# A softmax ranked behind the values of an older block, and two product steps moved ahead of two transposes

## The chip, the cores and the metric

The kernel runs on one core of a Trainium2 chip. Its time is the time of one execution on the device in microseconds (us); several runs are made and their median is compared. One further execution is recorded by the hardware profiler, and the rows below come from that one.

## The reference

The program is a transformer trunk of two layers on 1024 tokens of width 1024, in float32. Layer 0 is gated retention. Layer 1, which the change touches, is gated differential attention with 8 heads: each head has two queries and two keys per token (64 numbers each) and one value (128 numbers). Cut to that layer:

```python
h  = rmsnorm(x, pre_norm[1])
kv = rmsnorm(x, kv_norm) @ w_kv           # two keys and one value per head
k, v = rope(kv[..., :1024]), kv[..., 1024:]
q, gate = rope((h @ w_in_b)[..., :1024]), (h @ w_in_b)[..., 1024:]
# per head, per block of 128 queries; keys of later 64-token chunks are masked
p = softmax(where(mask, q_t @ k_t.T / 8, -big))        # t = 0, 1
o = (p[0] - lam * p[1]) @ v
o = rmsnorm(o, sub_norm) * (1 - lambda_init)
x = x + rmsnorm((o * silu(gate)) @ w_out_b, post_norm[1])
```

## The kernel before

Every product of an activation with a weight is made as three matmuls on operands that are split into a high and a low part (`split` makes them: ScalarE writes the high part, L87 or L90, VectorE subtracts, L88 or L91; `mm3` issues the three matmuls, L100). Layer 1 begins about two thirds into the run.

Its main loop goes over 64 units, heads outside (8), blocks of 128 tokens inside (8). A unit projects q, k and v of its block: eight slabs of three matmuls with 384 columns (`gemm_piece`, L100, the tile `pq` in the "g" banks of PSUM). Then `rotate_b` applies the rotary tables: two products on VectorE (L566, L567), their sum on GpSimd (L568), and ScalarE copies v (L569). The unit also carries, in between its slabs, work of earlier blocks:

- behind slab 1, piece 0 of the attention, `scores` of the block two units back: matmuls with 64 rows for both score sets (L591) into the two buffers of PSUM tag "s2". A block b has (b + 1) x 128 keys, so block 5 has 768, block 6 has 896 and block 7 has 1024. In the same function stands the softmax: for each of the two score sets a memset of the masked corner (L597), the maximum on VectorE (L598) and the exponential on ScalarE (L599, with its sum); then reciprocal, factor and the combination of both sets (L601, L602, L604).
- behind slab 3, piece 1, `values` of the block scored two units earlier: matmuls of the turned weights with v (L627) into a buffer of tag "s", which ScalarE copies out with a scale (L630) and squares (L631); L105 on VectorE and L106 on GpSimd make the inverse root, L633 applies it, L634 stores the result.
- behind slab 4, `transpose_b`: two transposes of the q and k of the unit before (L577) into tag "s", which are split into `qk` (L87, L88); the next unit's scores read them.
- behind slabs 5 and 7, pieces 2 and 3, `turn` of the block scored one unit earlier: transposes of its weights (L616) into tag "s", copied by ScalarE (L617).

Tag "s" has two buffers, so the four pieces that use it pass them on to each other; tag "s2" has two, which the two score sets of one block fill.

`ahead` asks for weight slabs of the next head, at slab 0 of the units of blocks 1 to 4, and at slabs 0 to 3 of the unit of block 7; each is a load, two splits on ScalarE (L90) and two on VectorE (L91), into 12 buffers that the current head's slabs leave one by one. In the last head `load_wob` loads the output weights instead, whose splits are 1024 wide.

What sets the order on the engines: the library's planner goes through the instructions before the run and puts each on its engine's queue when it reckons it ready; among those that are ready together the one that the code asks for first goes first. On the chip the queues then run in that order. Buffers are handed on when their last reader has finished.

After the loop comes the output product: `outs` yields after each of its steps, a step being three matmuls of 512 columns; 16 steps make 128 rows of the output, eight steps for each bank of tag "g". Some steps are taken before the last `transpose_b`, then three after each remaining piece of the attention, and the rest at the end:

```python
    og_ = outs()
    for _ in range(4):
        next(og_)
    transpose_b(*prev)
    for step in att:
        for p in step:
            p()
            for _ in range(3):
                next(og_, None)
```

Of the kernel before, what the change touches and what calls it, by code (L numbers as in the profile page):

```python
# [35 lines left out]
def yoco_kernel(ctx: ExitStack, tc: tile.TileContext, a: dict):  # L36
# [16 lines left out]
    def sbuf(tag, shape, dt, nm):  # L53
        return sb.tile(shape, dt, name=f"{nm}_{next(uid)}", tag=tag, bufs=BUFS[tag])
# [13 lines left out]
    def kt(shape, nm, dt=F32):  # L68
        return sbuf("k", shape, dt, nm)

    def sm(n):
        return sbuf("m", [P, n], F32, "m")
# [3 lines left out]
    def ps(tag, n=512):  # L76
        return psum.tile([P, n], F32, name=f"p{tag}_{next(uid)}", tag=tag, bufs=PB[tag])
# [25 lines left out]
    def rsqrt(out, in_, mul, add, n=1):  # L103
        t = sm(n)
        nc.vector.tensor_scalar(out=t, in0=in_, scalar1=mul, scalar2=add, op0=ALU.mult, op1=ALU.add)  # L105
        nc.gpsimd.tensor_tensor(out=out, in0=t, in1=mhalf[:, 0:n], op=ALU.pow)  # L106
# [295 lines left out]
    for i in range(H * NC):  # L402
# [3 lines left out]
        u = {"h": h, "c": c, "wg": wg, "pp": ps("s2", 1024)}  # L406
# [174 lines left out]
    def scores(u):  # L581
        h, b, nk = u["h"], u["b"], u["nk"]
        q, qs = groups[h, b // 4][0][:, 0], slice(b % 4 * P, b % 4 * P + P)
        sc = [ps("s2", 1024) for t in range(2)]
        for c0 in range(0, nk, 512):
            n = min(512, nk - c0)
            k = groups[h, c0 // 512][0][:, 1]
            for i, (ql, kl) in enumerate(((0, 0), (0, 1), (1, 0))):
                for t in range(2):
                    rows = slice(t * 64, t * 64 + 64)  # L590
                    nc.tensor.matmul(  # L591
                        sc[t][:, c0 : c0 + n], q[rows, ql, qs], k[rows, kl, 0:n], start=(i == 0), stop=(i == 2)
                    )
        nm, s_ = sm(2), sm(2)
        pr = [kt([P, D], f"pr{t}") for t in range(2)]
        for t in range(2):
            nc.vector.memset(sc[t][0:64, nk - 64 : nk], NEG)  # L597
            nc.vector.tensor_reduce(out=nm[:, t : t + 1], in_=sc[t][:, :nk], axis=AX.X, op=ALU.max, negate=True)  # L598
            nc.scalar.activation(pr[t][:, :nk], sc[t][:, :nk], AF.Exp, bias=nm[:, t : t + 1], accum_out=s_[:, t : t + 1])  # L599
        rc, cf = sm(2), sm(1)  # L600
        nc.vector.reciprocal(rc, s_)  # L601
        nc.vector.tensor_scalar(out=cf, in0=s_[:, 0:1], scalar1=rc[:, 1:2], scalar2=nlam, op0=ALU.mult, op1=ALU.mult)  # L602
        w = pr[0][:, :nk]
        nc.vector.scalar_tensor_tensor(out=w, in0=pr[1][:, :nk], scalar=cf, in1=w, op0=ALU.mult, op1=ALU.add)  # L604
        u.update(w=w, rc=rc)

    def turn(u, i):
        w = u["w"]
        if i == 0:
            u["wT"] = kt([P, D], "wT")  # L610
        k0, k1 = i * 512, min(u["nk"], i * 512 + 512)
        if k0 >= k1:
            return
        pt = ps("s")
        for k in range(k0, k1, P):
            nc.tensor.transpose(pt[:, k - k0 : k - k0 + P], w[:, k : k + P], ident)  # L616
        nc.scalar.activation(u["wT"][:, k0:k1], pt[:, : k1 - k0], AF.Copy)  # L617
# [3 lines left out]
    def values(u):  # L621
        h, b, wT, rc = u["h"], u["b"], u["wT"], u["rc"]
        valued.add((h, b))
        po = ps("s", P)
        for kb in range(b + 1):
            v = groups[h, kb // 4][1]
            nc.tensor.matmul(po, wT[:, kb * P : (kb + 1) * P], v[:, kb % 4], start=(kb == 0), stop=(kb == b))  # L627
        o = sbuf("u", [P, 2, P], F32, "o")
        sq, r = sm(1), sm(1)
        nc.scalar.activation(o[:, 0], po, AF.Copy, scale=rc[:, 0:1])  # L630
        nc.scalar.activation(o[:, 1], o[:, 0], AF.Square, accum_out=sq)  # L631
        rsqrt(r, sq, 1.0 / P, EPS)
        nc.gpsimd.tensor_tensor(out=o[:, 1], in0=o[:, 0], in1=r.to_broadcast([P, P]), op=ALU.mult)  # L633
        nc.sync.dma_start(og2d[b * P : (b + 1) * P, h * P : (h + 1) * P], o[:, 1])  # L634

    def attend(blocks):

        blocks = [{"h": h, "b": b, "nk": (b + 1) * P} for h, b in blocks]
        a_, b_ = None, None
        for u in blocks + [None, None]:  # L640
            pieces = []
            if u:
                pieces.append(lambda: scores(u))
            if a_:
                pieces.append(lambda: values(a_))
            if b_:
                pieces.append(lambda: turn(b_, 0))
                if b_["nk"] > 512:
                    pieces.append(lambda: turn(b_, 1))
            yield pieces  # L650
            a_, b_ = b_, u
# [59 lines left out]
    def outs():  # L711

        for t in range(NC):
            if t + 1 < NC:
                out_fetch(t + 1)
            for step, _ in enumerate(out_gemm(t)):
                if t + 1 < NC and step in (7, 11):
                    out_turn(t + 1, step // 8)
                yield

    LAG = 2
    att = attend([(h, b) for h in range(H) for b in range(NC)])
    prev = None
    for i in range(H * NC):
# [3 lines left out]
        pieces = next(att) if i >= LAG else []  # L728
# [21 lines left out]
        load_wob(f, wt([P, D], "wobh"), wt([P, D], "wobl"))  # L750
    spare = xt([P, 512], "spare", F32)
    og_ = outs()
    for _ in range(4):
        next(og_)
    transpose_b(*prev)
    for step in att:
# [91 lines left out]
```

## Time and profile before

| what | value |
|---|---|
| three runs | 1499.16, 1499.98, 1504.51 us, median 1499.98 |
| profiled execution: time | 1502.49 us |
| its span | 1500.70 us |
| PE (matmuls) busy | 1480.1 us, 99% of the span |
| PEld (weight loads) busy | 1296.2 us, 86% |
| VectorE busy | 786.4 us, 52% |
| ScalarE busy | 630.2 us, 42% |
| GpSimd busy | 270.4 us, 18% |
| TensorE clock granted | 0.998 of full speed over the run |

The span is the time from the first to the last instruction; the execution's own time is 1.79 us longer. Engines are PE (TensorE's matmuls), PEld (its weight loads, which overlap with matmuls), DVE (VectorE), ACT (ScalarE), POOL (GpSimd) and SP, which issues the DMAs. L599 is line 599 of the kernel. A wait is idle time of an engine ahead of an instruction, with what released it.

### The profile page before, as it was taken

The page shows a single profiled execution, that of the slowest core. Times are in us where ns is not written, and L with a number is a line of the kernel's source. Part 1 is how long each engine was busy: PE and PEld are TensorE (multiplying, and loading weights), DVE is VectorE, ACT ScalarE, POOL GpSimd, SP SyncE. Part 2 cuts the span into 40 slices and gives each one's busy share as a digit, 9 for nine tenths or more (in the row PEclk, how much of TensorE's full clock was granted, in tenths as well). Part 3 has the DMA queues.
Part 4 walks back from the last instruction along what each step waited for, and adds up shares of the span by engine and source line. Part 5 has one row for each costly group of instructions (what it writes and reads, how often), then busy time and mean ns, then how long its engine had stood idle before and what let it go on. Part 6 is the DMA issues. An engine that isn't in the chain of part 4 may idle for free.

```text
span 1500.7 us, 23837 instructions
## 1 busy us (share of the span) xinstructions
PE 1480.1 (99%) x8760; PEld 1296.2 (86%) x8760; DVE 786.4 (52%) x1991; ACT 630.2 (42%) x1611; POOL 270.4 (18%) x470
## 2 busy tenths in 40 slices
PE   8999999999999999999999999999999999999998
PEld 6888899988989888988888888988988988888886
DVE  5763545454545544541155501667567577577543
ACT  5642424242423332332244513556456465466421
POOL 0322122212222222200000000122222222222100
PEclk9999999999999999999999999999999999999999
DMA  7540302020211212243345512111011011013342
GB/s 256 162 119 15 99 15 89 22 85 29 60 53 47 64 45 76 71 172 112 135 161 182 182 67 78 31 41 52 11 51 52 11 52 46 16 66 137 121 167 98
DMA packets 71172, 125.63 MB, mean 84 GB/s; under 512 B 7696, under 2 KB 42384, under 8 KB 71056
## 3 DMA queue, kind: packets, MB, share of 16 engines
q1 hardware_dynamic: 70768, 123.85, 25.4%
q8 instruction: 69, 1.13, 0.3%
q14 instruction: 47, 0.39, 0.1%
q10 hardware_dynamic: 288, 0.26, 0.1%
HBM read 94.72 MB, written 29.36 MB: 83 GB/s over the span
## 4 chain that ended last, share of the span: by engine, by line
PE 84%; DVE 4%; issue 3%; ACT 3%; DMA 2%; POOL 1%; POOLq 0%; DVEq 0%; ACTq 0%; SPq 0%
PE pg L100 57%; PE ps L100 14%; PE ps L591 4%; PE ps L627 3%; PE ps L616 2%; PE ps L301 1%; DMA stg<-in_wa 1%; ACT pr L599 1%; DVE wbh L91 1%; PE ps L251 1%; PE ps L577 1%; DVE m L598 1%; PE ps L235 0%; PE ps L675 0%; PE ps L236 0%
## 5 line engine op out<-in xcount | busy, mean ns | idle before, releaser
L100 PE MATMUL pg<-wq,xT 128*128 128x512 f32 x1512 | 379.6, 400 | 0.0
L100 PE MATMUL pg<-wbh,x2T 128*128 128x384 f32 x1536 | 335.0, 353 | 0.0
L100 PEld LDWEIGHTS pg<-wq,xT 128*128 128x128 f32 x1512 | 275.4, 189 | 53.8 <-issue 0.5
L100 PEld LDWEIGHTS pg<-wbh,x2T 128*128 128x128 f32 x1536 | 256.3, 189 | 13.0 <-issue 9.3
L100 PE MATMUL ps<-wg,xT 128*128 128x256 f32 x1536 | 195.0, 283 | 0.0
L100 PEld LDWEIGHTS ps<-wg,xT 128*128 128x128 f32 x1536 | 189.1, 192 | 0.2
L106 POOL TENSOR_TENSOR m<-m,mhalf 128x1 f32<-128x1 f32 x144 | 79.7, 553 | 576.8 <-DVE m L105 500.8
L599 ACT ACTIVATE pr<-ps,m 128x256 f32<-128x256 f32 (+7 forms) x128 | 94.1, 738 | 91.0 <-DVE m L598 91.0
L218 POOL TENSOR_TENSOR a<-a 128x256 f32<-128x256 f32 x64 | 48.1, 752 | 324.7 <-DVE a L217 324.6
L598 DVE TENSOR_REDUCE m<-ps 128x1 f32<-128x256 f32 (+7 forms) x128 | 91.0, 752 | 0.0
L100 PE MATMUL pg<-wbg,x2T 128*128 128x512 f32 x384 | 88.4, 390 | 0.0
L90 ACT ACTIVATE r<-pg,tabA 128x256 fp32r<-128x256 f32 x63 | 29.7, 471 | 133.1 <-DVE a L217 129.8
L100 PEld LDWEIGHTS pg<-wbg,x2T 128*128 128x128 f32 x384 | 71.8, 188 | 14.8
L100 PEld LDWEIGHTS ps<-r,r 128*128 128x128 f32 x528 | 72.1, 191 | 9.7 <-ACT r L253 3.7
L252 DVE TENSOR_TENSOR a<-ps,tabA 128x128 f32<-128x128 f32 x64 | 18.5, 289 | 115.1 <-PE ps L251 113.1
L100 PE MATMUL ps<-r,r 128*128 128x256 f32 x528 | 74.8, 284 | 3.4 <-ACT r L253 2.5
L627 PE MATMUL ps<-v,wT 128*128 128x128 f32 x576 | 74.6, 275 | 0.2 <-DVE ps L597 0.2
L627 PEld LDWEIGHTS ps<-v,wT 128*128 128x128 f32 x576 | 73.1, 191 | 0.7 <-PE pg L100 0.5
L568 POOL TENSOR_TENSOR tabB<-tabB 128x256 f32<-128x256 f32 x64 | 49.6, 776 | 124.7 <-DVE tabB L567 124.4
L216 DVE TENSOR_TENSOR a<-pg,tabA 128x256 f32<-128x256 f32 x63 | 26.6, 422 | 78.3 <-PE pg L100 78.3
L253 ACT ACTIVATE r<-a 128x128 fp32r<-128x128 f32 x64 | 19.8, 309 | 106.5 <-DVE a L252 106.5
L100 PE MATMUL pg<-wo,oh 128*128 128x512 f32 x192 | 60.8, 398 | 1.1 <-ACT oh L87 1.1
(158 smaller groups left out, 2387.0 us busy)
## 6 DMA issues: line engine op xcount, KB each, us to landing
stw<-in_wa SPq DMA_DIRECT2D x56, 256.0 KB, 3.0
stb<-in_wbh SPq DMA_DIRECT2D x64, 192.0 KB, 2.4
xr<-in_x SPq DMA_DIRECT2D x16, 512.0 KB, 4.4
stg<-in_wa SPq DMA_DIRECT2D x32, 256.0 KB, 3.3
ogd<-a SPq DMA_DIRECT2D x64, 128.0 KB, 1.9
sto<-in_woa SPq DMA_DIRECT2D x16, 512.0 KB, 3.7
og<-ogd SPq DMA_DIRECT2D x16, 512.0 KB, 4.1
y0d<-y SPq DMA_DIRECT2D x8, 512.0 KB, 2.9
```

The costliest lines, as they stand in the source:

```text
L90: nc.scalar.activation(hi, src, AF.Copy, scale=scale)
L100: nc.tensor.matmul(out, l, r, start=(first and i == 0), stop=(last and i == n - 1))
L106: nc.gpsimd.tensor_tensor(out=out, in0=t, in1=mhalf[:, 0:n], op=ALU.pow)
L216: nc.vector.tensor_tensor(out=o4(t1), in0=q4, in1=cb, op=ALU.mult)
L218: nc.gpsimd.tensor_tensor(out=qk, in0=t1, in1=t2, op=ALU.add)
L253: nc.scalar.activation(ss[:, 0, :], sc, AF.Copy)
L568: nc.gpsimd.tensor_tensor(out=r[:, 2], in0=r[:, 0], in1=r[:, 1], op=ALU.add)
L591: nc.tensor.matmul(sc[t][:, c0 : c0 + n], q[rows, ql, qs], k[rows, kl, 0:n], start=(i == 0), stop=(i == 2))
L598: nc.vector.tensor_reduce(out=nm[:, t : t + 1], in_=sc[t][:, :nk], axis=AX.X, op=ALU.max, negate=True)
L599: nc.scalar.activation(pr[t][:, :nk], sc[t][:, :nk], AF.Exp, bias=nm[:, t : t + 1], accum_out=s_[:, t : t + 1])
L616: nc.tensor.transpose(pt[:, k - k0 : k - k0 + P], w[:, k : k + P], ident)
L627: nc.tensor.matmul(po, wT[:, kb * P : (kb + 1) * P], v[:, kb % 4], start=(kb == 0), stop=(kb == b))
```

## The change

The function `scores` is cut in two. Its matmuls stay where they are, behind slab 1; its softmax becomes a function of its own that is called behind slab 3, after `values` of the older block and in the same piece. The pieces behind slabs 5 and 7 stay. In the tail six steps of the output product instead of four are taken before the last `transpose_b`.

```diff
@@ in scores(u), behind the score matmuls
+        u["sc"] = sc
+
+    def softmax(u):
+        nk, sc = u["nk"], u["sc"]
         nm, s_ = sm(2), sm(2)
         pr = [kt([P, D], f"pr{t}") for t in range(2)]
         for t in range(2):
@@ in attend(blocks)
             if u:
                 pieces.append(lambda: scores(u))
-            if a_:
-                pieces.append(lambda: values(a_))
+
+            pieces.append(lambda: [f(x) for f, x in ((values, a_), (softmax, u)) if x])
             if b_:
                 pieces.append(lambda: turn(b_, 0))
@@ in the tail
     og_ = outs()
-    for _ in range(4):
+    for _ in range(6):
         next(og_)
     transpose_b(*prev)
```

## Rows read from the trace of the kernel before

**Rows 1.** Waits of PE, whole run: total us, times, longest us.

```profile
PE ps L616 <- ACT o L630: 4.8, 9, 0.9
...
PE ps L577 <- POOL tabB L568: 0.7, 1, 0.7
```

**Rows 2.** Waits of all engines, 930 to 1500.7 us: total us, times, longest us.

```profile
ACT pr L599 <- DVE m L598: 91.0, 55, 3.0
...
DVE ps L597 <- PE ps L591: 49.3, 46, 1.4
...
PEld ps L616 <- ACT o L630: 9.2, 16, 1.2
...
PEld ps L616 <- ACT wT L617: 2.2, 6, 0.4
```

**Rows 3.** Timeline, scoring block 6: start, us, engine, line, tiles, count [idle before].

```profile
1038.33 0.47 DVE L91 SCALAR_TENSOR_TENSOR wbh<-stb,gains,wbh 128x256 fp32r<-128x256 f32 x1
...
1038.50 1.28 PE L627 MATMUL ps<-v,wT 128*128 128x128 f32 x10
...
1038.96 2.09 DVE L598 TENSOR_REDUCE m<-ps 128x1 f32<-128x896 f32 x2
...
1040.15 1.01 ACT L599 ACTIVATE pr<-ps,m 128x896 f32<-128x896 f32 x1 [1.94 <-DVE m L598]
...
1040.28 0.77 PE L100 MATMUL pg<-wbh,x2T 128*128 128x384 f32 x3
...
1041.15 0.36 ACT L630 ACTIVATE o<-ps,m 128x128 f32<-128x128 f32 x1
...
1041.40 1.01 ACT L599 ACTIVATE pr<-ps,m 128x896 f32<-128x896 f32 x1
1041.56 0.42 PEld L616 LDWEIGHTS ps<-ident,pr 128*128 128x128 f32 x4 [0.82 <-ACT o L630]
...
1041.97 1.31 PE L100 MATMUL pg<-wbh,x2T 128*128 128x384 f32 x6
```

**Rows 4.** Timeline of the next unit, which scores block 7, and the scores behind it.

```profile
1046.47 0.18 DVE L597 MEMSET ps<- 64x64 f32 x2 [1.35 <-PE ps L591]
...
1049.08 0.37 ACT L630 ACTIVATE o<-ps,m 128x128 f32<-128x128 f32 x1
...
1049.50 0.77 PE L100 MATMUL pg<-wbh,x2T 128*128 128x384 f32 x3
...
1050.35 0.20 ACT L599 ACTIVATION_READ_ACCUMULATOR pr<-ps,m 128x1 f32 x1
...
1050.46 1.31 PE L100 MATMUL pg<-wbh,x2T 128*128 128x384 f32 x6
...
1053.10 0.55 PE L591 MATMUL ps<-qk 64*128 64x128 f32 x6
```

**Rows 5.** Timeline, the unit that scores block 5, in the same head.

```profile
1033.31 0.51 ACT L90 ACTIVATE wbh<-stb,gains 128x256 fp32r<-128x256 f32 x1
...
1033.71 0.36 ACT L630 ACTIVATE o<-ps,m 128x128 f32<-128x128 f32 x1
...
1034.12 0.42 PEld L616 LDWEIGHTS ps<-ident,pr 128*128 128x128 f32 x4 [0.23 <-ACT o L630]
...
1035.90 0.53 PEld L591 LDWEIGHTS ps<-qk,qk 64*128 64x128 f32 x6 [0.18 <-DVE qk L88]
```

**Rows 6.** Timeline, last head, the unit that scores block 4.

```profile
1374.63 1.15 ACT L90 ACTIVATE wob<-sto,gsub 128x1024 fp32r<-128x1024 f32 x1 [2.48 <-DMA sto<-in_wob]
...
1376.87 0.66 PE L616 MATMUL ps<-ident,pr 128*128 128x128 f32 x4 [0.52 <-ACT o L630]
```

**Rows 7.** Timeline, the product's first steps and the last q/k transposes.

```profile
1387.57 2.98 PE L100 MATMUL pg<-wob,wo 128*128 128x512 f32 x12
...
1390.50 0.72 POOL L568 TENSOR_TENSOR tabB<-tabB 128x256 f32<-128x256 f32 x1
...
1391.28 0.44 PE L577 MATMUL ps<-ident,tabB 128*128 128x128 f32 x2 [0.73 <-POOL tabB L568]
```

## The prediction

> **What bounds the kernel now.** I read the table of busy shares first: TensorE is busy 99% of 1500.70 us, so only time in which TensorE waits can be won. Next the list of who waited for whom. In the whole run PE waits for the copy of the values' result (L630 on ScalarE) 4.8 us in nine waits, all before the transposes of the weights (L616), and once 0.7 us for GpSimd's rotary sum (L568) before the last q/k transposes (L577) [rows 1]. Nothing else that the change touches is in that list. The change can therefore win some microseconds out of 1500, and the question is how many of them, and whether it makes new waits.
>
> How long the nine waits are is not plain. The same list for the weight loads has 9.2 us behind L630 and 2.2 us more behind L617 [rows 2], against 4.8 us on the matmul row. The skill (the Trainium skill, Perfetto Trace Analysis, section Identifying the Most-Contended Engine) holds matmul busy time for a bad measure, since matmuls are pipelined, and sends the reader to the weight loads; by it the prize is 9.2 us, by the matmul row 4.8 us. I take neither but the spacing of starts. In the unit that scores block 6 (896 keys) the three matmuls ahead of the transposes start at 1040.28 and the six behind them at 1041.97, 1.69 us apart; where nothing waits, in the next unit, the same stretch takes from 1049.50 to 1050.46, 0.96 us [rows 3, 4]. So that wait costs 0.73 us, between the matmul row and the 0.82 us of the weight load.
>
> The timeline of that unit says where the wait comes from [rows 3]. The weight splits (L91) hold VectorE until 1038.80, so the two maxima (L598) start only then, the first exponential (L599) starts at 1040.15 and ends with its accumulator read near 1041.1; only then does ScalarE copy the values' result (L630, 1041.15), though the values' matmuls were through at 1039.78. The transposes need the PSUM buffer which that copy empties. The pattern stands seven times, once for block 6 of each of the heads 0 to 6; the other two of the nine waits are in the last head's projections, where wide weight splits are in the way.
>
> One more thing the rows show, and the forecast hangs on it: the engines do not run in the order of the code. The code asks for both exponentials ahead of the copy, yet ScalarE runs exponential, copy, exponential; and the L91 splits were asked for units later than the maxima that they precede [rows 3]. So the library orders each engine by what it reckons ready first, and the code's order decides only between instructions that are ready together.
>
> **The change, part by part.** No instruction is added or removed: the 64 softmaxes and 64 value steps keep their work, and no DMA is touched. What moves is the rank of the softmax: memsets, maxima, exponentials, reciprocal and combination now rank behind the older block's value matmuls, L630, L631, L105 and the store of its result, and behind whatever weight splits the two projection slabs in between ask for.
>
> (a) Units where VectorE and ScalarE are free when the scores end. In 46 of the 62 units VectorE sat idle until the scores arrived (49.3 us in all), and in 55 cases ScalarE sat idle until the maximum (91.0 us) [rows 2]. The softmax is then the only thing ready, rank or no rank: six projection matmuls (1.31 us) and the values' own matmuls lie between the scores and the copy. Cost and gain nothing; the idle engines are the cover. If that cover were gone (order strictly by rank) it would be rival D.
>
> (b) The seven block-6 units. Does the copy now get ahead of the first exponential? In time on the chip both are ready almost together (1039.78 against 1040.15), which speaks for a swap. But the order is fixed beforehand by the library's reckoning, and its order tells what that was: it gave VectorE splits that rank below the maxima, so in its view the scores had not ended when it did so, and VectorE was free at most one split (0.47 us) after them. Add memset 0.18 and one maximum 1.05 (half of 2.09): first exponential ready some 1.7 us after the scores. The copy is ready after six projection matmuls, 1.31, and ten value passes, 1.28: 2.6 us [rows 3, 4]. With ScalarE idle at 1.7 us the exponential goes first under either rank, and the seven waits stay. Bounds for this part: 0, and all of it, 6 x 0.73 plus about 1.0 for the longest (0.9 on the matmul row, [rows 1]) is 5.4 us, plus at most 2.2 us of waits behind L617 that follow from a late copy [rows 2], of which I count 1.3. I take 0, since the order in the rows is on that side.
>
> (c) The seven units before them, which score block 5 while new weights are split. There ScalarE is full, so rank decides. Now both exponentials and then a split (L90, 1033.31) precede the copy (1033.71), the weight load of the transposes waits 0.23 us, and the next scores wait 0.18 us for the k split (L88) [rows 5]. The copy and that split will now come ahead of the second exponential. Bounds: both waits go, 0.41 x 7 = 2.9 us at most; or the combination L604 delays L88 by the split's 0.51 and the copy's 0.36, 0.9 x 7 = 6 us lost. VectorE picks by readiness again, and the later the softmax, the freer it is for L88. The weight loads' waits mostly hide in the matmul before them (the PE list has none for these), so I take 1.0 us won.
>
> (d) Last head. Before block 4 a wide split (L90, 1.15 us) holds ScalarE while values and maximum both become ready, so here rank should decide and the 0.52 us wait goes [rows 6]. The remaining late one (4.8 less this and the seven) may go too, 0 to 0.5 us. I take 0.6 us for both.
>
> (e) Two more steps in front of the last transposes: six matmuls of 512 columns. In the row of twelve they take 2.98/12 = 0.25 us each, 1.5 us for six. PE now ends its twelve at 1390.55 and waits until 1391.28, 0.73 us, for the sum that GpSimd ends at 1391.22 [rows 7]. The six cover the whole wait; nothing is late next, because the steps are taken from later in the same product and the accumulator (eight steps a bank) is not passed. The scores behind them start later by 1.5 - 0.73 us, which other product steps cover. Gain 0.7 us; lower bound 0, if the sum came later too.
>
> Sum: 0 + 0 + 1.0 + 0.6 + 0.7 = 2.3 us. The profiled execution had a span of 1500.70 and a time of 1502.49, 1.79 around it; the span becomes 1498.4 and that execution 1500.2. The median of the runs shown is 1499.98, 2.51 below the profiled one, so I forecast 1499.98 - 2.3 = **1497.7 us**.
>
> **Rivals.**
> B, the copies get ahead everywhere: (b) comes out at its other end, 5.4 + 1.3 more, 9.0 us together, 1491.0 us. For it: on the chip copy and exponential are ready within 0.4 us of each other [rows 3]. Against it: the reckoning in (b).
> C, nothing moves but the tail: ranks decide nowhere, and the wait for the rotary sum is won: 1499.3 us. For it: the idle engines of (a).
> D, slower. The engines' queues really follow the new rank, so memsets and maxima stand behind the values' copy, square and L105 in every unit. In the unit that scores block 7 the memset moves from 1046.47 to behind the copy, which ends at 1049.45: 2.98 us. Its last accumulator read then ends at 1053.53 instead of 1050.55; the next scores start at 1053.10 and need the two score buffers that it empties [rows 4]. It decides once a softmax slips by more than 2.55 us; then at least 0.43 us a unit, in some three long blocks of eight heads, 10 us: 1510 us. The skill says that ScalarE and VectorE take their queues strictly in order (the Trainium skill, Perfetto Trace Analysis, section Tensor Engine Instruction), and the rows agree: L630, ready at 1039.78, stands behind the exponential until 1041.15 [rows 3]; so if the library did queue a waiting L105 ahead of the memsets, everything behind it would stand. Against D: the rows show it filling idle engines by readiness.
>
> **How the numbers follow.** Forecast 0.58, B 0.20, C 0.14, D 0.08. Half a per cent, 7.5 us, is about what a measurement of this kernel can tell from no change. Only B reaches it downwards, and not always, since 9.0 us is near the bound: faster 0.13. D reaches it upwards most of the time: slower 0.06. Same 0.81. The range takes in C and the loss bound of (c), and most of B: 1491.5 to 1502.5; D and the best of B are left out.
>
> **What would show it.** In the profile after: the wait of L577 for L568 gone; the wait of L616 for L630 still there seven times with about 0.7 us spacing lost, and still exponential, copy, exponential in the block-6 units (a copy ahead of both is B); in the block-5 units L630 ahead of the second exponential; VectorE's memsets still right behind the scores. Waits of L591 for L599 would be D. The forecast is wrong if the library's order in the block-6 units flips, or if a later L604 makes scores or transposes wait.

## The result and the profile after

| | before | after |
|---|---|---|
| median of 4 runs | 1499.91 us | 1509.42 us |
| lowest and highest | 1499.16, 1504.51 us | 1507.89, 1512.04 us |
| profiled execution: time, span | 1502.49, 1500.7 us | 1507.89, 1506.1 us |

The ratio is 1.0061 [1.0046, 1.0075]: the kernel became slower by 9.5 us, above the forecast's range (1491.5 to 1502.5 us) and the other way than forecast. The profiled spans are only 5.4 us apart, because the profiled execution of after was the fastest of its four and that of before 2.6 us above its median. What follows locates these 5.4 us; the other 4 us lie between executions, which one profile can't place.

The list of PE's waits over the whole run, after (total us, times, longest us), against [rows 1]:

```profile
PE ps L591 <- ACT pr L603: 2.3, 5, 0.8
...
PE ps L620 <- DVE wo L88: 0.6, 1, 0.6
PE ps L620 <- ACT o L634: 0.5, 1, 0.5
```

The wait of the transposes for the values' copy, nine times and 4.8 us before, stands once (L630 is now L634, L616 is L620). L577 <- L568 is gone. In their place the scores (L591) wait for the exponentials (L603), and one wait of 0.6 us for the low part of a split (L88) is new in the tail. By this list alone the change would have won, so it isn't the whole account. All engines, 930 to 1506 us, against [rows 2]:

```profile
DVE m L105 <- ACT o L635: 128.3, 59, 3.7
...
ACT pr L603 <- DVE m L602: 35.6, 49, 2.3
...
DVE ps L601 <- PE ps L591: 13.4, 16, 1.2
...
PEld ps L591 <- ACT pr L603: 11.2, 28, 1.1
```

The line of before that belongs to the first of these:

```profile
DVE m L105 <- ACT o L631: 22.5, 15, 3.6
```

These two lines are the change in one place. VectorE now stands 128.3 us, in 59 places, at L105, the first small step behind the values' square; in before the same wait was 22.5 us in 15 places. The time in which it stood ready for the scores fell from 49.3 us to 13.4, and ScalarE's wait for the maxima from 91.0 us to 35.6: not less idling, but idling in front of older work. The score matmuls' weight loads wait 28 times, 11.2 us.

The timeline of after, the unit that scores block 6 (start, us, engine, line, tiles, count [idle before]), against [rows 3]:

```profile
1035.08 0.29 PEld L591 LDWEIGHTS ps<-qk,qk 64*128 64x128 f32 x2 [0.24 <-ACT pr L603]
...
1035.96 0.29 PEld L591 LDWEIGHTS ps<-qk,qk 64*128 64x128 f32 x3 [0.59 <-ACT pr L603]
...
1037.37 1.31 PE L100 MATMUL pg<-wbh,x2T 128*128 128x384 f32 x6
...
1038.26 0.18 DVE L601 MEMSET ps<- 64x64 f32 x2
...
1039.89 0.37 ACT L634 ACTIVATE o<-ps,m 128x128 f32<-128x128 f32 x1 [1.78 <-issue]
...
1040.72 0.15 DVE L105 TENSOR_SCALAR m<-m 128x1 f32<-128x1 f32 x1 [1.03 <-ACT o L635]
...
1040.79 2.08 DVE L602 TENSOR_REDUCE m<-ps 128x1 f32<-128x896 f32 x2
...
1041.91 1.01 ACT L603 ACTIVATE pr<-ps,m 128x896 f32<-128x896 f32 x1 [0.94 <-DVE m L602]
```

The scores of block 6 themselves wait twice for the exponentials of block 5. The memsets still come behind the scores. The maxima do not: VectorE idles 1.03 us, does L105, and only then the maxima. The copy is ahead of both exponentials, which is what the forecast said would not happen in this unit. The next unit, which scores block 7, and the scores behind it, against [rows 4]:

```profile
1045.71 0.19 DVE L601 MEMSET ps<- 64x64 f32 x2
...
1048.39 0.37 ACT L634 ACTIVATE o<-ps,m 128x128 f32<-128x128 f32 x1 [3.46 <-issue]
...
1049.23 0.15 DVE L105 TENSOR_SCALAR m<-m 128x1 f32<-128x1 f32 x1 [3.33 <-ACT o L635]
...
1049.30 2.35 DVE L602 TENSOR_REDUCE m<-ps 128x1 f32<-128x1024 f32 x2
...
1052.03 0.18 PEld L591 LDWEIGHTS ps<-qk 64*128 64x128 f32 x1 [0.25 <-ACT pr L603]
...
1052.69 0.19 ACT L603 ACTIVATION_READ_ACCUMULATOR pr<-ps,m 128x1 f32 x1
...
1052.77 0.71 PE L591 MATMUL ps<-qk 64*128 64x128 f32 x5
...
1053.41 1.31 PE L100 MATMUL pg<-wbh,x2T 128*128 128x384 f32 x6
```

The last accumulator read ends at 1052.88, 7.17 us behind the memset; before it was 4.08 (1046.47 to 1050.55). The softmax slipped by 3.09 us, and the six score matmuls of the next block, 0.48 us from their start to the next projection before, take 1.38, split in two by the wait for each of the two score buffers.

Such intervals over all units make the account. One interval is the time from the first score matmul (L591) of a unit to that of the next, by the starts in the trace; the table has the median of heads 0 to 6 for each scored block, in us, and the sum for a head, with the experiments below beside it.

| block | 0 | 1 | 2 | 3 | 4 | 5 | 6 | 7 | head |
|---|---|---|---|---|---|---|---|---|---|
| before | 7.54 | 7.09 | 5.79 | 6.27 | 6.94 | 7.47 | 8.82 | 8.33 | 58.25 |
| after | 8.44 | 7.07 | 5.79 | 6.29 | 6.91 | 7.32 | 8.70 | 8.25 | 58.78 |
| e3 | 7.55 | 7.09 | 5.79 | 6.29 | 6.91 | 7.39 | 9.42 | 8.45 | 58.89 |
| e4 | 7.55 | 7.09 | 5.79 | 6.29 | 6.91 | 7.71 | 7.89 | 8.37 | 57.61 |
| e5 | 7.54 | 7.09 | 5.79 | 6.29 | 6.91 | 7.35 | 8.72 | 8.62 | 58.31 |
| e6 | 7.55 | 7.10 | 5.79 | 6.43 | 7.26 | 7.78 | 8.62 | 8.34 | 58.87 |
| e8 | 7.55 | 7.09 | 5.79 | 6.29 | 6.91 | 7.47 | 8.94 | 8.46 | 58.50 |
| e9 | 7.55 | 7.09 | 5.79 | 6.27 | 6.94 | 7.47 | 7.84 | 8.37 | 57.32 |

Summed over heads 0 to 6, after minus before: block 0 +5.39 (0.9 in each of the six heads that follow another), block 5 +1.66, block 6 -0.64, block 7 -0.63, blocks 1 to 4 -0.17. The last head, up to the first step of the output product, costs 0.40 us more (block 0 +0.91, block 2 -0.63, block 4 +0.90, block 5 up to that step -0.78). From that step to the last matmul it is 106.48 us instead of 106.58; by this stretch the two moved steps can be judged, which an interval from the last scores on can't do, since they bring 1.4 us of matmuls ahead of those. What lies ahead of the first scores is 1.12 us shorter, what follows the last matmul 0.64 us longer; together that is the 5.4 us. Block 5 is a sum of two signs: 0.13 to 0.16 us won in four heads and 0.04 in one, but 1.44 and 0.87 lost in heads 3 and 4.

The tail in the timeline, against [rows 7]:

```profile
1392.45 3.00 PE L100 MATMUL pg<-wob,wo 128*128 128x512 f32 x12
...
1394.28 0.75 POOL L568 TENSOR_TENSOR tabB<-tabB 128x256 f32<-128x256 f32 x1 [2.30 <-DVE tabB L567]
...
1396.64 0.38 PE L577 MATMUL ps<-ident,tabB 128*128 128x128 f32 x2
```

The sum ends at 1395.03, the transposes start at 1396.64 behind the six added matmuls, with no wait. The new wait for L88 stands 24 us further on.

### The profile page after: what moved, and what is told of

Its sections match the earlier page's. It is cut to its first block, busy times and chain, and to the rows that moved or that the text cites. A ratio compares the mean times of both kernels' runs of the same rounds, so it can differ in the third digit from the quotient of the medians.

```text
span 1506.1 us, 23824 instructions
## 1 busy us (share of the span) xinstructions
PE 1487.9 (99%) x8760; PEld 1304.4 (87%) x8760; DVE 782.2 (52%) x1991; ACT 631.6 (42%) x1611; POOL 272.4 (18%) x470
## 5 line engine op out<-in xcount | busy, mean ns | idle before, releaser
L603 ACT ACTIVATE pr<-ps,m 128x256 f32<-128x256 f32 (+7 forms) x128 | 93.9, 738 | 36.6 <-DVE m L602 35.6
L634 ACT ACTIVATE o<-ps,m 128x128 f32<-128x128 f32 x64 | 23.5, 368 | 149.6 <-issue 90.3
L568 POOL TENSOR_TENSOR tabB<-tabB 128x256 f32<-128x256 f32 x64 | 49.8, 779 | 200.5 <-DVE tabB L567 177.5
L105 DVE TENSOR_SCALAR m<-m 128x1 f32<-128x1 f32 x88 | 13.5, 153 | 135.3 <-ACT o L635 128.3
```

The source lines that it names most:

```text
L568: nc.gpsimd.tensor_tensor(out=r[:, 2], in0=r[:, 0], in1=r[:, 1], op=ALU.add)
```

## The experiments

The small tiles of a row's numbers come from one pool of 48 buffers, the tag "m": the maxima `nm` and sums `s_` of the softmax, and the square's sum, its root and L105's result of the values. Theory T: the planner hands out a tag's buffers in the order in which the code asks for them. An instruction can't be put on its queue before it has its buffer, however idle its engine is; so a softmax asked for behind the values has its maxima placed behind L105 in every unit. The rivals: the tail steps or rank alone did it; or the order of the score matmuls (both sets in turn, so that the wait of one delays the other) makes the loss.

**e1 and e2, the two parts alone.**

```diff
# e1: after, without the tail's two steps
-    for _ in range(6):
+    for _ in range(4):
# e2: before, with them
-    for _ in range(4):
+    for _ in range(6):
```

> The softmax moved as in the change, four product steps ahead of the last transposes as before. Theory S (the softmax's new place costs): as slow as the changed kernel, 1507 to 1511 us, with the scores L591 waiting some 11 us on the weight-load row for the exponentials. Rival W (the two moved product steps cost): back near 1500 us.

> The kernel before with six product steps instead of four. Theory S: 0.3 to 0.7 us faster than before (the wait of L577 for the rotary sum gone), so 1499 to 1500 us and not to be told from before. Rival W: 1507 us or more.

e1: 1509.86 us against 1502.04 of before, ratio 1.0051 [1.0039, 1.0064]. e2: 1499.88 us, 0.999 [0.9981, 0.9999]. The softmax alone is as slow as the whole change, so the loss is the softmax's. The tail's steps alone win 1.5 us by the ratio (0.15 to 2.9), and 0.96 us from the product's first step to the last matmul (105.62 us instead of 106.58). In e1, without them, that stretch takes 105.79 us and has no wait for L568: the new place of the softmax had removed this wait already.

**e3, buffers of their own for maxima and sums.** After, with one difference: the softmax's small tiles come from another tag.

```diff
-    BUFS = {..., "m": 48, "u": 3}
+    BUFS = {..., "m": 48, "u": 3, "n": 12}
+    def sn(n):
+        return sbuf("n", [P, n], F32, "n")
-        nm, s_ = sm(2), sm(2)
+        nm, s_ = sn(2), sn(2)
```

> The changed kernel, but the tiles for the two maxima and the two sums of the softmax come from a buffer tag of their own instead of the tag m that they share with the values' small tiles. Theory T (the maxima stand behind L105 because a tag hands its buffers out in the order of the code, so the maximum cannot be placed until the older block's small tiles have been): the maxima stand right behind the scores again, the scores wait for no exponential, 1495 to 1500 us. Rival R (the rank itself holds the maxima back, whatever buffers they write): L105 still ahead of the maxima, 1507 to 1511 us.

1507.67 us, ratio 1.0041 [1.0027, 1.0055]. Timeline of the block-6 unit of e3 (its lines are three further down):

```profile
1098.08 2.09 DVE L605 TENSOR_REDUCE n<-ps 128x1 f32<-128x896 f32 x2
...
1099.08 0.77 PE L103 MATMUL pg<-wbh,x2T 128*128 128x384 f32 x3
1099.27 1.01 ACT L606 ACTIVATE pr<-ps,n 128x896 f32<-128x896 f32 x1 [1.80 <-DVE n L605]
...
1100.26 0.36 ACT L637 ACTIVATE o<-ps,m 128x128 f32<-128x128 f32 x1
...
1101.09 1.29 PE L103 MATMUL pg<-wbh,x2T 128*128 128x384 f32 x6
...
1102.72 0.44 PE L623 MATMUL ps<-ident,pr 128*128 128x128 f32 x2 [0.34 <-ACT wT L624]
```

The mechanism came out as T has it: the maxima are back behind the memset (which starts at 1097.93), no score waits for an exponential, and block 0 has its 7.55 us again. The time did not. With free buffers the planner puts exponential, copy, exponential again, and the copy is later still: the stretch from the three projection matmuls to the six takes 2.01 us (1.69 before, 0.96 without a wait), and behind it the second set of transposes waits for L624. The 0.32 us more than in before are VectorE's: splits (L94) hold it longer, so that the maxima start 1.00 us ahead of those three matmuls (1098.08 and 1099.08) instead of 1.32 (1038.96 and 1040.28, [rows 3]), and exponential and copy follow them at the same distance as in before. PE's waits in e3:

```profile
PE ps L623 <- ACT o L637: 7.1, 7, 2.2
PE ps L623 <- ACT wT L624: 3.1, 7, 1.2
```

So T explains why the maxima and with them the next scores were late, and the expectation that this was the only price of the new rank (1495 to 1500 us) failed. The old wait comes back larger (block 6 at 9.42 us, 0.60 above before), and the last head's block 4 takes 11.35 us instead of 8.11.

**e4, maxima early, exponentials late.** After, with `nm`, the memsets and the maxima back in `scores`; sums, exponentials and combination stay behind the values.

```diff
         # in scores(u)
+        nm = sm(2)
+        for t in range(2):
+            nc.vector.memset(sc[t][0:64, nk - 64 : nk], NEG)
+            nc.vector.tensor_reduce(out=nm[:, t : t + 1], ...)
+        u.update(sc=sc, nm=nm)
     def softmax(u):
-        nm, s_ = sm(2), sm(2)
+        s_ = sm(2)
```

> Memsets and maxima asked for in scores as before, only the exponentials and what follows behind the values; six product steps. Theory S with T: the maxima run right behind the scores, the copy and square of the values stand ahead of both exponentials in every unit, so the transposes' wait for the copy goes (5.4 us, and about 1 us behind it) while the exponentials come 0.6 us (block 6) to 1.8 us (block 7) later than before, inside the 2.5 us that block 7 has: 1491 to 1496 us. Rival X (any exponential behind the values' copy is too late for the next scores): the scores wait as in the changed kernel, 1503 us or more.

1498.71 us, ratio 0.9979 [0.9971, 0.9988]: faster than before by 3.3 us, less than the 1491 to 1496 us expected. The copy is ahead of both exponentials, VectorE has its maxima early, and block 6 falls to 7.89 us. Block 5 pays 0.24 for it, and block 4 of the last head takes 9.82 us instead of 8.11.

**e5, only block 7's softmax where it was.** After, with the softmax called in the scores' piece for block 7.

```diff
-                pieces.append(lambda: scores(u))
+                pieces.append(lambda: [f(u) for f in
+                    ((scores, softmax) if u["b"] == 7 else (scores,))])
 # ... behind the values: the softmax of the other blocks only
```

> The changed kernel, with the softmax of block 7 alone back in scores. Theory S (the loss is made where the long softmax of block 7 ends too late for the scores of the next head's block 0): the interval from the scores of block 0 to those of block 1 goes back from 8.45 to about 7.55 us, 0.9 us in each of seven heads, so some 6 us below the changed kernel, within 3 us of before. Rival R (the late softmaxes of all blocks cost a little each): under 2 us below the changed kernel.

1506.19 us, ratio 1.0025 [1.0015, 1.0034]. Block 0's interval is back at 7.54 us, so its 0.9 us a head was the late softmax of block 7 and nothing else. The time came down by 5.4 us by the two ratios (1.0061 and 1.0025) and by 3.2 by the medians, where 6 were expected; rival R's 2 us fail. It stays 4.0 us above before, not within 3: in the profile of e5 the blocks 5, 6 and 7 of heads 0 to 6 cost 2.79, 0.73 and 1.89 us more than in before.

**e6, the score pairs one set after the other.** Before, with the two loops of `scores` exchanged.

```diff
-            for i, (ql, kl) in enumerate(((0, 0), (0, 1), (1, 0))):
-                for t in range(2):
+            for t in range(2):
+                for i, (ql, kl) in enumerate(((0, 0), (0, 1), (1, 0))):
```

> The kernel before with the two loops of the score matmuls exchanged: three matmuls of the first score set, then three of the second, instead of in turn. No wait is added. If two 64-row matmuls that stand next to each other and write different sets run side by side, each 512 columns of three pairs take some 0.7 us longer, 6 us a head, 40 to 50 us in all. If they do not, the time stays within 2 us of before.

1508.39 us, ratio 1.0039 [1.0027, 1.0051]: slower by 6.2 us, where less than 2 or more than 40 were expected. Timeline of block 7's scores in e6, and its wait for the copy:

```profile
1045.22 0.97 PE L591 MATMUL ps<-qk,qk 64*128 64x512 f32 x6
...
1046.02 0.86 PE L591 MATMUL ps<-qk 64*128 64x512 f32 x6
...
1046.82 0.45 PE L100 MATMUL pg<-wbh,x2T 128*128 128x384 f32 x1
```

```profile
PE ps L616 <- ACT o L630: 6.9, 16, 2.5
```

From the first score to the next projection it is 1.60 us, against 1.59 in before: PE doesn't mind the order. But the planner then orders the other engines differently. In the eight block-4 units the copy, which stood between the two exponentials, now stands behind both; in the block-5 units a weight split stands between the two maxima and another between the two exponentials, so that the second exponential starts 0.30 us later behind the scores (4.30 us instead of 4.00), and the seven new waits for the copy, 0.2 us each, are there. That the pairs' order by itself costs PE time is refuted; whether it makes the wait for two buffers in after longer, no run shows.

**e7, e4 with the last head as before.**

```diff
-                pieces.append(lambda: scores(u))
+                pieces.append(lambda: [f(u) for f in
+                    ((scores, softmax) if u["h"] == H - 1 else (scores,))])
 # ... behind the values: the softmax of the other heads only
```

> The kernel with early maxima and late exponentials for heads 0 to 6, and in the last head the whole softmax in scores as before; six product steps. Theory: the gain of seven heads stays, and the unit of block 4 in the last head goes back from 9.8 towards 8.1 us: 4 to 6 us faster than before. Rival: the last head's loss comes from the six steps or from elsewhere; then as the early-maxima kernel, 3 us faster than before.

1499.48 us, ratio 0.9982 [0.9974, 0.9991], as e4: the rival's time. Block 4 of the last head fell to 7.37 us and block 5 rose to 13.41 (11.37 in e4). What the last head pays, it pays at one place or the other; why is not shown.

**e8, e4 with the sums in buffers of their own.** The sharpest test of T: the maxima are early as in e4, the rank of the exponentials is e4's, only the sums' tag differs.

```diff
-        s_ = sm(2)
+        s_ = sn(2)          # tag "n", 6 buffers
```

> The early-maxima kernel, with the tile of the two sums, which the exponentials write, taken from a tag of its own. Theory T (the exponentials stand behind the values' copy and square because their sums' tile comes from the tag of the values' small tiles): the first exponential goes ahead of the copy again in the block 6 units, the transposes wait for the copy as before, and the time is within 2 us of before. Rival R (the rank alone puts the copy first): as the early-maxima kernel, about 3 us faster than before.

1504.73 us, ratio 1.0013 [1.0004, 1.0021]. PE's waits and the block-6 unit's timeline in e8:

```profile
PE ps L625 <- ACT o L639: 4.3, 7, 2.1
...
PE ps L625 <- ACT wT L626: 2.4, 7, 0.5
```

```profile
1041.82 1.01 ACT L608 ACTIVATE pr<-ps,m 128x896 f32<-128x896 f32 x1 [1.29 <-DVE m L600]
...
1042.82 0.36 ACT L639 ACTIVATE o<-ps,m 128x128 f32<-128x128 f32 x1
```

The time is 2.6 us above before, where at most 2 were expected. The exponential is ahead of the copy again, block 6 takes 8.94 us instead of 7.89. Where the sums lie decides the order, not where the exponentials stand in the code. It does so in the whole loop, which has 62 units with older values: the copy stands ahead of both exponentials in all 62 of after, e1 and e4, in none of before, in one of e3 and in one of e8; the maxima stand behind the older block's L105 in all 62 of after and e1, and in none of before, e3, e4 and e8.

**e9 and e10, the late exponentials only where they win.** e9 is e4 with the exponentials late for block 6 of heads 0 to 6 alone; e10 adds block 4 of the last head, the place of [rows 6].

```diff
+                late = u["b"] == 6 and u["h"] < H - 1
+                pieces.append(lambda: [f(u) for f in
+                    ((scores,) if late else (scores, softmax))])
 # ... behind the values: the softmax only if late
 # e10
+                late = (...) or (u["h"], u["b"]) == (H - 1, 4)
```

> Early maxima everywhere, late exponentials in block 6 of heads 0 to 6 alone, all other softmaxes whole and in scores as before; six product steps. Theory: block 6's interval falls from 8.8 to about 7.9 us as in the early-maxima kernel, block 5's stays at 7.5 us, and the last head stays as before: seven times 0.9 us and the tail's share, 6 to 8 us faster than before, the fastest so far. Rival: the gain in block 6 needs the late exponentials of block 5, whose splits then end earlier; without them under 3 us.

> As the kernel with block 6 alone, and block 4 of the last head late too, where a wide weight split holds ScalarE. If the copy can go first there, the wait of 0.5 us goes (the interval 8.1 us falls to about 7.5 us); if the late exponentials are what made that interval 9.8 us in the early-maxima kernel, it rises by 1 to 2 us.

e9: 1492.93 us (1490.17 to 1494.56) against 1502.23 of before, ratio 0.994 [0.9926, 0.9953]. It beats both kernels, and by more than the 6 to 8 us expected: 9.3 us by the medians, of which the profile shows 6.9 in block 6 and 0.96 from the product's first step to the last matmul. Timeline of its block-6 unit:

```profile
1036.14 2.09 DVE L597 TENSOR_REDUCE m<-ps 128x1 f32<-128x896 f32 x2
...
1037.02 0.37 ACT L636 ACTIVATE o<-ps,m 128x128 f32<-128x128 f32 x1 [1.01 <-issue]
...
1037.43 0.77 PE L100 MATMUL pg<-wbh,x2T 128*128 128x384 f32 x3
...
1037.99 1.01 ACT L605 ACTIVATE pr<-ps,m 128x896 f32<-128x896 f32 x1
1038.04 0.60 PE L622 MATMUL ps<-ident,pr 128*128 128x128 f32 x4
...
1038.40 1.30 PE L100 MATMUL pg<-wbh,x2T 128*128 128x384 f32 x6
```

Copy first, both exponentials behind it, the transposes without a wait, and 0.97 us from the three projection matmuls to the six: the free spacing of [rows 4]. Block 6 takes 7.84 us, 0.98 less than before, in each of seven heads; no other block pays more than 0.04 us. e10: 1494.94 us, 0.9953 [0.9941, 0.9966]; block 4 of the last head takes 9.19 us instead of 7.96 in e9. The copy is ahead of both exponentials there, and yet the transposes wait 1.60 us for it (0.38 in e9): it stands behind a second wide split, which itself waits 0.73 us for its weights. The same is seen in that unit of after:

```profile
1380.17 1.15 ACT L90 ACTIVATE wob<-sto,gsub 128x1024 fp32r<-128x1024 f32 x1 [1.10 <-DMA sto<-in_wob]
1381.23 0.35 ACT L634 ACTIVATE o<-ps,m 128x128 f32<-128x128 f32 x1
```

## Why the prediction was wrong

**(a), the step that failed.** It put the cost at nothing: "the softmax is then the only thing ready, rank or no rank". Ready also means having a buffer. The maxima's tile comes from the tag that the values' small tiles share, and that, not an engine's load, put the maxima behind L105: in e3 they come at once with another tag, in e4 with the same tag and an earlier rank; e8 shows the same of the exponentials and their sums. The 46 idle waits for the scores and the 55 for the maxima [rows 2], taken as cover, were the slack that the new order used up: 59 waits at L105 took their place. In the short blocks it costs nothing, as forecast (blocks 1 to 4 moved by -0.17 us together); in block 7 it does, and 5.4 us of the loss stand in the interval that follows it, 0.9 in each of six heads (and 0.9 more in the last head). That the whole measured 9.5 us come from it is not shown: e5, which takes this part away, is still 4.0 us slower than before.

**Rival D had the right order, with a chance of 0.08.** It put the maxima behind copy, square and L105 and got a slip of 2.98 us; measured 3.09. Its reason, queues that follow the new rank, was not the right one: e3 has the same rank with other buffers, and there the maxima are early. It took the memset for the instruction that slips; that one stayed, since the score buffer it writes is already held. Its price, at least 0.43 us a unit, was half of the measured 0.9. Its 1510 us met 1509.42 largely by luck: three long blocks were to lose alike, but only the place behind block 7 lost net, and the profiles hold 5.4 of the 9.5 us. The Trainium skill (Perfetto Trace Analysis, section Tensor Engine Instruction) has VectorE take its queue strictly in order, and the rows of after agree: the scores were there, and the maxima stood behind a waiting L105 for 1.03 and 3.33 us. The argument against D, that the rows show idle engines filled by readiness, held in before, and by T only because there the softmax's tiles were asked for ahead of the values'.

**(b)** had the order wrong and came near its 0 us by luck. Its reckoning of 1.7 against 2.6 us fits kernels in which nothing gates the softmax: e3, with buffers apart, has exponential, copy, exponential under the new rank. In after the maxima came late, and the copy went first. But the win was eaten: block 6's scores themselves wait for block 5's exponentials and take 2.28 us instead of 1.42 from their start to the next projection; 0.86 lost against the 0.98 that e9 shows the reordering to be worth leaves the measured 0.12. The size of the prize was right: 5.4 us and the 1.3 counted behind L617 make 6.7, and e9 wins 7 x 0.98 = 6.9 us in these units, 0.72 each at the first set of transposes and the rest at the second, which is freed too. For the first set the spacing, 0.73, was the better measure than the weight load's 0.82 [rows 3]; the preference for weight loads over matmul busy time that the prediction took from the Trainium skill (Perfetto Trace Analysis, section Identifying the Most-Contended Engine) is one for judging busy time, not for sizing a wait.

**(c)** had its sign right in five heads (0.13 to 0.16 us in four of them; the forecast's 1.0 over seven is 0.14) and missed the two in which block 5 lost 1.44 and 0.87 us. There ScalarE waited for weights that landed late (last section), with the exponentials now behind that split instead of ahead of it.

**(d)** met its size by luck. Without block 0, the last head up to the product's first step gained 0.51 us against the 0.6 forecast, but not where it was forecast: the wait before block 4 stayed (0.52 us before, 0.53 in after) and that block lost 0.90; block 2 won 0.63 and block 5 0.78. What failed is that rank decides there: in after the copy is ahead of both exponentials, and what holds it is a wide split that waits 1.10 us for its weights.

**(e)** holds for the steps alone: in e2 the wait for L568 is gone and 0.96 us are won, 0.7 forecast. In after it failed: the sum ends before the first twelve matmuls do, so the wait that the steps were to cover had gone already, and with the new wait of 0.63 us for L88 the stretch is 0.69 us longer than in e1, which lacks the steps. That the steps cause this wait is not shown; e3 and e5 have them and not the wait.

Open: the 4 us between the medians' difference and the profiles'; and why block 7 costs 0.29 us a head more in e5 than in before.

## What to carry to other kernels

Where a planner hands out a pool's buffers in the order of the code, moving code moves the place of its tiles in that pool, and an idle engine is no cover: before putting the cost of a move at nothing, list which buffers the moved instructions take and which older ones now come first. To put one instruction behind another, split the step at the tile that gates it: here the maximum stays early and only the exponential goes behind the copy. Make the move only in the units where the trace shows the wait: in every unit it lost 9.5 us whole and won 3.3 with the exponentials alone; in seven of 64 units, and with the tail's steps, these won 9.3. And look first at what else stands ahead on the engine: e10 made the move at one more such wait, behind a wide split, and that unit lost 1.2 us.

## What the runs showed of the hardware

Neither the issue of one DMA on SP nor its way from issue to landing is a constant. For L494, the weight slabs' load, in after (instruction, count, ns min/median/max; then us from issue to landing, min/median/max):

```profile
L494 SPq DMA_DIRECT2D stb<-in_wbh x64: 327/328/1504, 856.2 to 1277.7; - x64
...
DMA to landing us min/median/max: 2.2/2.5/4.2
```

In heads 3 and 4, the two heads in which block 5 lost, the first of four loads was issued as fast as elsewhere (333 ns) but landed 4.00 and 3.42 us later, 2.36 in head 2. In the timeline of after, head 3:

```profile
1151.50 0.40 ACT L90 ACTIVATE wbh<-stb,gq 128x128 fp32r<-128x128 f32 x1 [1.89 <-PE pg L100]
...
1153.16 0.89 ACT L603 ACTIVATE pr<-ps,m 128x768 f32<-128x768 f32 x1
...
1154.19 0.29 PEld L591 LDWEIGHTS ps<-qk,qk 64*128 64x128 f32 x2 [1.15 <-ACT pr L603]
```

That load was issued at 1147.41 and landed at 1151.41. ScalarE stands 1.89 us ahead of the split and starts it 0.09 us behind the landing (the row's named releaser, a projection matmul, had long been done); the exponential is queued behind it, and the next scores' weight load waits 1.15 us. In head 4 ScalarE stands 1.31 us, in head 2 0.24. So it stands 1.64 and 1.06 us longer than in head 2, and block 5 takes 1.61 and 1.03 us longer. In before the same loads of heads 3 and 4 took 3.79 and 4.08 us, but the exponentials stood ahead of the split, which started 0.96 and 0.68 us behind the landing: there the late landing cost nothing.

What goes with a late landing is a fetch of instructions on the DMA queues. Between 1147 and 1152 us of after they show:

```profile
q8 instruction: 1, 0.02, 1.9%
```

One packet of 16 KB, from 1148.43 to 1149.98. Over the loads for heads 2 to 7 in all twelve traces, 106 had such a packet under way between issue and landing, with a median of 3.3 us (2.3 to 4.8), and 470 had none, with a median of 2.4 (2.2 to 3.9). Long issues go with it too: over 0.4 us took 18 of the 38 issues with such a packet under way, the 1504 ns among them, and 5 of the 538 others. That the packet is the cause is inferred; no run moves it.

And the twelve score matmuls of block 7, on 64 rows and 512 columns each, take 1.59 us from the first to the next projection with the sets in turn and 1.60 us one set after the other (e6).
